# A hybrid decoder step on one Trainium2 core: first loads reordered, key copies moved, 512-column projections, 256 and 320 token columns

## Chip, cores and metric

The kernel runs as one program on one core of a Trainium2 chip. The metric is device time in microseconds of one execution. The profile is one execution, taken by the hardware profiler; its span runs from the first to the last instruction.

## The reference, cut to what matters

One layer of a decoder trunk is computed for 1024 prompt tokens and 64 sample tokens (8 sequences of 8), width 1024, FFN width 2816, all in float32.

```python
h = rmsnorm(x, norm_mix)
proj = h @ w_in                      # q/k/v for a gated DeltaNet, its gates, q/k/v for window attention
o_a = rmsnorm(gated_delta_rule(causal_conv(...)), norm_out_a) * silu(z)     # 4 heads of 128
o_b = rmsnorm(combine_by_denominator(dilated branches), norm_out_b)         # 8 heads of 64
x = x + concat([o_a, o_b]) @ w_out
hf = rmsnorm(x, norm_ffn)
x = x + (silu(hf @ w_gate) * (hf @ w_up)) @ w_down
y = rmsnorm(x, norm_final)
```

The sample tokens attend over a cache of 2048 keys and values per sequence. Among the outputs are the caches moved on by eight rows (`new_wk_sample`, `new_wv_sample`), 32 MB of copies each; part of them goes out from tiles that the attention has loaded, the rest as copies from DRAM to DRAM.

## The kernel before, in words

**Tokens and stages.** The prompt is cut into two groups G (or F in the second half of the kernel): group 0 has 512 prompt tokens, group 1 the other 512; the 64 sample tokens go with group 0 in the input projections and with group 1 in the output projection and the FFN. A tile of tokens is 128 rows; the sample tile has 64. The stages follow one another: norm and input projections (`norm_in`, `proj_a`, `proj_b`), the DeltaNet beside them, attention and the first half of the output projection (`outproj_a`, mixed heads 0 to 3), then `outproj_b(0)`, `ffn_norm(0)`, `ffn(0)` with attention of group 1 and the decode attention (`decode_k`, `decode_v`) beside it, and at the end `outproj_b(1)`, `ffn_norm(1)`, `ffn(1)`, alone but for copies.

**Matmuls.** Each float32 operand is split into a high and a low float32r part: `split` (lines 222 to 224) rounds on ScalarE and subtracts on VectorE. A product is then three matmuls: high by high, high by low, low by high, all issued on line 198. `dense_T` holds 128 weight columns still and streams n tokens, 24 matmuls of n columns for a depth of 1024. `nat_mm` holds 128 tokens still and streams weight columns, 12 matmuls for four blocks of depth (8 for the 64 sample tokens).

**Weights.** `wload` (line 226) loads 512 KB raw into one of two buffers (`WB`), `wsplit` (line 231) splits it into one of three high and three low buffers (`WH`, `WL`), or into four buffers of another pool when `own` is given.

**The FFN** (`ffn`, line 1261) goes over the 22 blocks of 128 FFN columns in groups of four (one group of two). Per block it loads gate and up weights and calls `dense_T` twice for each entry of `cols`: (0, 512) for F = 0, (0, 288) and (288, 288) for F = 1. From the two banks ScalarE and VectorE make the SwiGLU product (lines 1293 to 1298). After a group, `down` (line 1313) adds the group's product with `w_down` to the residual `x2` in SBUF: for each column part c and each token tile 12 matmuls into one PSUM bank, then one VectorE eviction on line 1320. For F = 0 and a group of four the column part is 256 wide (`ncol`), four parts; otherwise 512, two parts. `outproj_b` (line 1218) is built the same way, four parts of 256, its eviction on line 1238. In the stages up to the first FFN two banks (`m=2`) serve all these products; `ffn(1)` has six.

**The norm before the FFN** (`ffn_norm`, line 1250) goes by token tile through `norm_T` (line 284): a sum of squares on ScalarE (288), eight small VectorE steps (214 to 219), a scaled multiply (289), eight transposes on TensorE against the identity (294), two splits. The first norm of the kernel (`norm_in`) is the same with `wmix`.

**The order of work.** Generators yield estimated costs; `beside` takes turns between a main stream and side streams by a pace, so that matmuls of attention stand between those of the FFN. The framework then orders each engine's queue by priority and data, so that an instruction without predecessors may come far ahead of its place in the text: the eight copies of the last 512 key rows per sequence (line 1026, 1 MB each, issued by GpSimd, written inside `decode_k`) leave in the first 150 us.

**The first loads** (lines 1412 to 1418) go out on SP's queue in this order: two x tiles, the table of constants `tab` (520 KB, with the identity for transposes as its first 128 columns), `wmix` (one row broadcast to 128 partitions, 512 KB), the first weight, three more x tiles.

**The last copies.** `far_rows` (line 1338) copies the far part of a cache, 1.5 MB per sequence, from SP's queue in program order, beside `outproj_b(1)` and `ffn(1)` for the values, at a pace of 4.5 per copy and 0.3.

```python
            last, wide = f + nb == nf, F or nb == 2
            ncol = 512 if wide else 256
            parts = nb * ncol // 1024
            ...
    x0 = list(load_in(0, npl, range(2)))
    sp.dma_start(tab, C["table"])
    wbc = bcast_row(npl, I["norm_mix"], "wmix")
    raws = [(i, wload(in_cols(i), 8, 128)) for i in IN_ORDER[:E1]]
```

Of the kernel before, what the change touches and what calls it, by code (L numbers as in the profile page):

```python
# [86 lines left out]
def consts():  # L87
# [6 lines left out]
    t["ident"] = p == c  # L94
# [43 lines left out]
    return off, {"table": table, "wb": wb, "dbias": np.ascontiguousarray(db_all), "xin": xin}  # L138
# [8 lines left out]
def body(tc, I, O, C, off):  # L147
# [21 lines left out]
    def K(name):  # L169
        o, n = off[name]  # L170
        return tab[:, o:o + n]

    ident, ii, utri, ones = K("ident"), K("ii"), K("utri"), K("ones")
# [20 lines left out]
    def mbank():  # L194
        return bank("m", "pm")
# [795 lines left out]
    def decode_k(tp, pairs, kb=2, kt_=3, qb=2, pb=1):  # L991
# [23 lines left out]
        for pi in pairs:  # L1015
            S = tp.tile([96, 2, 64], F32, name="S", tag="S", bufs=1)
            pa = obank()
            for s in range(2):
                b = 2 * pi + s
                c16, o16, c4, o4, src = cache_rows(I["cache_win_k"], O["new_wk_sample"], b)  # L1020
                for j in range(4):
                    for i in range(2):
                        hs = slice(i * 64, i * 64 + 64)
                        nc.gpsimd.tensor_copy(qbd[hs, s, j, 2 * j + i::8], qf[hs, j, b * 8:(b + 1) * 8])
                n = PAST - 512
                pool_q.dma_start(O["new_wk_sample"][0, b, n - DS:PAST - DS].rearrange("(a e) h d -> a (e h d)", a=64),
                                 I["cache_win_k"][0, b, n:PAST].rearrange("(a e) h d -> a (e h d)", a=64))
# [192 lines left out]
    def outproj_b(F, tp, x2):  # L1220
# [11 lines left out]
        for c in range(4):  # L1232
            w = wsplit(w_out[:, 4:8, c * 256:(c + 1) * 256], 4, 256)
            for i, rows, col in toks(F):
                ps = mbank()[:, :256]
                nat_mm(his(hi), his(lo), w, 4, rows, col, ps, True, True)
                xv = x2[:, col // 128, c * 256:(c + 1) * 256]
                dve.tensor_tensor(xv, ps, xv, op=OP.add)  # L1238
                yield 1.3
# [21 lines left out]
    def ffn(F, tp, x2, hp):  # L1261
        cols = [(0, 288), (288, 288)] if F else [(0, 512)]
# [19 lines left out]
        while f < nf:  # L1282
# [3 lines left out]
            for j in range(nb):  # L1286
                wg = wsplit(w_g[:, :, (f + j) * 128:(f + j + 1) * 128], 8, 128)
                wu = wsplit(w_u[:, :, (f + j) * 128:(f + j + 1) * 128], 8, 128)
                for c0, n in cols:
                    pg = yield from dense_T(*wg, hi, lo, c0, n)  # L1290
                    pu = yield from dense_T(*wu, hi, lo, c0, n)
                    th = hp.tile([128, 512], F32, name="hth", bufs=2)[:, :n]
                    act.activation(th, pg[:, :n], AF.Tanh, scale=0.5)  # L1293
                    dve.scalar_tensor_tensor(th, th, 1.0, pg[:, :n], op0=OP.add, op1=OP.mult)
                    dve.tensor_tensor(th, th, pu[:, :n], op=OP.mult)
                    act.activation(hh[j][:, c0:c0 + n], th, AF.Copy, scale=0.5)
                    m = min(n, 512 - c0)
                    dve.scalar_tensor_tensor(hl[j][:, c0:c0 + m], th[:, :m], 0.5, hh[j][:, c0:c0 + m].bitcast(F32),
                                             op0=OP.mult, op1=OP.subtract)
                    if m < n:  # L1300
                        dve.scalar_tensor_tensor(hh[j][:, 576:640], th[:, m:n], 0.5, hh[j][:, 512:576].bitcast(F32),
                                                 op0=OP.mult, op1=OP.subtract)
                yield 0.1
            last, wide = f + nb == nf, F or nb == 2
            ncol = 512 if wide else 256
# [33 lines left out]
    def far_rows(c, o, new):  # L1339
# [5 lines left out]
        sp.dma_start(o[0, :, PAST - DS:PAST].rearrange("b t h d -> b t (h d)"), new.rearrange("(b t) f -> b t f", t=DS))  # L1345

# [66 lines left out]
    sp.dma_start(tab, C["table"])  # L1413
    wbc = bcast_row(npl, I["norm_mix"], "wmix")
    raws = [(i, wload(in_cols(i), 8, 128)) for i in IN_ORDER[:E1]]
    x0 += load_in(0, npl, range(2, 5))
    raws += [(i, wload(in_cols(i), 8, 128)) for i in IN_ORDER[E1:E2]]
# [74 lines left out]
    far = Side(far_rows(I["cache_win_v"], O["new_wv_sample"], smp[2]))  # L1492
# [31 lines left out]
```

## Time and profile before

| | us |
|---|---|
| median of 3 runs | 1782.13 (1782.08 to 1786.56) |
| the profiled execution, device time | 1786.49 |
| its span | 1784.7 |
| TensorE busy | 1697.0 (95%) |
| VectorE busy | 1150.2 (64%) |
| ScalarE busy | 679.4 (38%) |

All times below are microseconds from the start of the span unless another unit stands there. PE is TensorE's matmuls, PEld its weight loads, DVE is VectorE, ACT ScalarE, POOL GpSimd, SP the engine that only issues transfers; a q behind the name means the engine's queue of issues. A name such as x<-pm,x reads: tile x written from pm and x. In brackets stands how long the engine was idle before, and what ended the wait. The ends of matmuls are modelled, so that the distance between starts is the better measure of their cost.

### The profile page before, as it was taken

The page shows a single profiled execution, that of the slowest core. Times are in us where ns is not written, and L with a number is a line of the kernel's source. Part 1 is how long each engine was busy: PE and PEld are TensorE (multiplying, and loading weights), DVE is VectorE, ACT ScalarE, POOL GpSimd, SP SyncE. Part 2 cuts the span into 40 slices and gives each one's busy share as a digit, 9 for nine tenths or more (in the row PEclk, how much of TensorE's full clock was granted, in tenths as well). Part 3 has the DMA queues.
Part 4 walks back from the last instruction along what each step waited for, and adds up shares of the span by engine and source line. Part 5 has one row for each costly group of instructions (what it writes and reads, how often), then busy time and mean ns, then how long its engine had stood idle before and what let it go on. Part 6 is the DMA issues. An engine that isn't in the chain of part 4 may idle for free. (4 is left out here: it accounts for less than half of the span.)

```text
span 1784.7 us, 27958 instructions
## 1 busy us (share of the span) xinstructions
PE 1697.0 (95%) x10462; PEld 1464.7 (82%) x10462; DVE 1150.2 (64%) x2829; ACT 679.4 (38%) x1379; POOL 78.2 (4%) x200
## 2 busy tenths in 40 slices
PE   4999999997999999999999989999998999999997
PEld 4988789996766668878887778888887999999996
DVE  6978966866776757797666546676576444343435
ACT  4545434441423353676421134454234223131222
POOL 1000000001001000000011001111100000000000
PEclk9999999998999999999998999999998999999999
DMA  8645556468898867534299678798494333241321
GB/s 272 182 145 159 162 179 171 116 200 271 266 282 256 256 208 225 188 104 118 66 284 287 180 224 256 248 304 274 133 325 154 128 95 95 59 130 36 107 72 65
DMA packets 309569, 324.96 MB, mean 182 GB/s; under 512 B 28221, under 2 KB 260669, under 8 KB 307754
## 3 DMA queue, kind: packets, MB, share of 16 engines
q1 hardware_dynamic: 297754, 275.64, 51.6%
q0 software_dynamic: 10304, 43.08, 6.8%
q10 hardware_dynamic: 1376, 4.46, 0.7%
q8 instruction: 82, 1.34, 0.3%
q14 instruction: 53, 0.43, 0.1%
HBM read 251.31 MB, written 105.63 MB: 200 GB/s over the span
## 5 line engine op out<-in xcount | busy, mean ns | idle before, releaser
L198 PE MATMUL pm<-act_hi,whi 128*128 128x288 f32 (+1 forms) x1056 | 349.4, 331 | 0.2 <-ACT act_hi L223 0.2
L198 PE MATMUL pm<-act_lo,whi 128*128 128x288 f32 (+1 forms) x1056 | 348.1, 330 | 0.0
L198 PE MATMUL pm<-act_hi,wlo 128*128 128x288 f32 (+1 forms) x1056 | 347.4, 329 | 0.0
L223 ACT ACTIVATE whi<-wraw 128x1024 fp32r<-128x1024 f32 x182 | 192.8, 1059 | 381.8 <-PE pm L198 275.8
L224 DVE TENSOR_TENSOR wlo<-wraw,whi 128x1024 fp32r<-128x1024 f32 x182 | 222.3, 1222 | 123.8 <-ACT whi L223 123.3
L198 PE MATMUL pm<-xh,whi 128*128 128x320 f32 (+2 forms) x672 | 230.6, 343 | 11.5 <-ACT whi L223 8.6
L198 PE MATMUL pm<-xl,whi 128*128 128x320 f32 (+2 forms) x672 | 228.4, 340 | 0.1
L198 PE MATMUL pm<-xh,wlo 128*128 128x320 f32 (+2 forms) x672 | 226.7, 338 | 0.2
L198 PEld LDWEIGHTS pm<-act_hi,whi 128*128 128x128 f32 x1056 | 199.2, 189 | 18.4 <-issue 2.1
L198 PEld LDWEIGHTS pm<-act_hi,wlo 128*128 128x128 f32 x1056 | 199.3, 189 | 14.5 <-issue 0.5
L198 PEld LDWEIGHTS pm<-act_lo,whi 128*128 128x128 f32 x1056 | 199.3, 189 | 14.2 <-issue 0.2
L198 PEld LDWEIGHTS pm<-xh,whi 128*128 128x128 f32 x672 | 129.1, 192 | 25.9 <-ACT whi L223 9.1
L1320 DVE TENSOR_TENSOR x<-pm,x 128x256 f32<-128x256 f32 (+1 forms) x148 | 79.9, 543 | 98.2 <-PE pm L198 97.8
L198 PEld LDWEIGHTS pm<-xl,whi 128*128 128x128 f32 x672 | 129.0, 192 | 11.9 <-issue 3.2
L198 PEld LDWEIGHTS pm<-xh,wlo 128*128 128x128 f32 x672 | 128.7, 192 | 10.6 <-DVE wlo L224 1.5
L198 PE MATMUL pm<-own,hh 128*128 128x512 f32 x440 | 129.4, 390 | 0.0
L198 PE MATMUL pm<-whi,hh 128*128 128x256 f32 (+1 forms) x336 | 101.6, 303 | 12.9 <-DVE x L1320 7.6
L198 PE MATMUL pm<-whi,hl 128*128 128x256 f32 (+1 forms) x336 | 99.7, 299 | 0.0
L198 PE MATMUL pm<-wlo,hh 128*128 128x256 f32 (+1 forms) x336 | 99.4, 297 | 0.0
L198 PEld LDWEIGHTS pm<-own,hh 128*128 128x128 f32 x440 | 82.2, 188 | 16.9 <-issue 0.2
L198 PE MATMUL pm<-whi,nat_hi 128*128 128x256 f32 x288 | 83.4, 293 | 1.5 <-DVE n_ss L219 1.1
L1293 ACT ACTIVATE hth<-pm 128x288 f32<-128x288 f32 (+1 forms) x66 | 30.5, 462 | 139.4 <-PE pm L198 139.3
(362 smaller groups left out, 3180.9 us busy)
## 6 DMA issues: line engine op xcount, KB each, us to landing
wraw<-w_in SPq DMA_DIRECT2D x56, 512.0 KB, 4.6
wraw<-w_gate SPq DMA_DIRECT2D x44, 512.0 KB, 3.7
wraw<-w_up SPq DMA_DIRECT2D x44, 512.0 KB, 3.8
wraw<-w_down SPq DMA_DIRECT2D x44, 512.0 KB, 3.6
new_wk_sample<-cache_win_k SPq DMA_DIRECT2D x8, 1536.0 KB, 8.2
qbc<-smp SPq DMA_DIRECT2D x32, 384.0 KB, 7.2
kt<-cache_win_k SPq DMA_DIRECT2D x32, 384.0 KB, 7.0
vt<-cache_win_v SPq DMA_DIRECT2D x32, 384.0 KB, 4.2
```

What stands on the lines that cost most here:

```text
L198: pe.matmul(out, lhsT, rhs, start=start, stop=stop)
L223: act.activation(hi, src, AF.Copy)
L224: dve.tensor_sub(lo, src, hi.bitcast(F32))
L1293: act.activation(th, pg[:, :n], AF.Tanh, scale=0.5)
L1320: dve.tensor_tensor(xv, ps, xv, op=OP.add)
```

## The change

Four things are edited. The identity becomes a tensor and a load of its own, and the loads go out as x tiles, `wmix`, identity, first weight, x tiles, table. The eight key copies leave `decode_k` and GpSimd's queue and become a generator `near_keys` on SP's queue, in program order, behind the far values. The down projection always uses 512 columns, and `outproj_b` does too; a group of four blocks then takes its weights for one half in two pieces of two blocks. The second FFN cuts its tokens into 256 and 320, and its first group (two blocks) does both blocks for the first 256 tokens before the other 320, with the second block's weights in the pool's own buffers.

```diff
-    t["ident"] = p == c
...
-    ident, ii, utri, ones = K("ident"), K("ii"), K("utri"), K("ones")
+    ident = cp.tile([128, 128], F32, name="ident")
+    ii, utri, ones = K("ii"), K("utri"), K("ones")
...
-                n = PAST - 512
-                pool_q.dma_start(O["new_wk_sample"][0, b, n - DS:PAST - DS].rearrange("(a e) h d -> a (e h d)", a=64),
-                                 I["cache_win_k"][0, b, n:PAST].rearrange("(a e) h d -> a (e h d)", a=64))
...
-        for c in range(4):
-            w = wsplit(w_out[:, 4:8, c * 256:(c + 1) * 256], 4, 256)
+        for c in range(2):
+            cs = slice(c * 512, (c + 1) * 512)
+            w = [wsplit(w_out[:, k:k + 2, cs], 2, 512) for k in (4, 6)]
             for i, rows, col in toks(F):
-                ps = mbank()[:, :256]
-                nat_mm(his(hi), his(lo), w, 4, rows, col, ps, True, True)
-                xv = x2[:, col // 128, c * 256:(c + 1) * 256]
+                ps = mbank()
+                for q in range(2):
+                    nat_mm(his(hi), his(lo), w[q], 2, rows, col, ps, q == 0, q == 1, 2 * q)
+                xv = x2[:, col // 128, cs]
                 dve.tensor_tensor(xv, ps, xv, op=OP.add)
-                yield 1.3
+                yield 2.6
...
-        cols = [(0, 288), (288, 288)] if F else [(0, 512)]
+        cols = [(0, 256), (256, 320)] if F else [(0, 512)]
...
-            for j in range(nb):
-                wg = wsplit(w_g[:, :, (f + j) * 128:(f + j + 1) * 128], 8, 128)
-                wu = wsplit(w_u[:, :, (f + j) * 128:(f + j + 1) * 128], 8, 128)
-                for c0, n in cols:
...
+            early = F and f == 0
+            ws = {}
+            for j, (c0, n) in ([(j, c) for c in cols for j in range(nb)] if early else [(j, c) for j in range(nb) for c in cols]):
+                if j not in ws:
+                    ws = ws if early else {}
+                    ws[j] = [wsplit(x[:, :, (f + j) * 128:(f + j + 1) * 128], 8, 128, own=hp if early and j else None)
+                             for x in (w_g, w_u)]
+                wg, wu = ws[j]
+                pg = yield from dense_T(*wg, hi, lo, c0, n)
+                pu = yield from dense_T(*wu, hi, lo, c0, n)
...
-            last, wide = f + nb == nf, F or nb == 2
-            ncol = 512 if wide else 256
+            last, ncol = f + nb == nf, 512
...
+    def near_keys():
+
+        n = PAST - 512
+        for b in range(DB):
+            d_, s_ = (x[0, b, r:r + 512].rearrange("(a e) h d -> a (e h d)", a=64) for x, r in
+                      ((O["new_wk_sample"], n - DS), (I["cache_win_k"], n)))
+            tc.keep_in_program_order(sp.dma_start(d_, s_))
+            yield 4.5
...
     x0 = list(load_in(0, npl, range(2)))
-    sp.dma_start(tab, C["table"])
     wbc = bcast_row(npl, I["norm_mix"], "wmix")
+    sp.dma_start(ident, C["ident"])
     raws = [(i, wload(in_cols(i), 8, 128)) for i in IN_ORDER[:E1]]
     x0 += load_in(0, npl, range(2, 5))
+    sp.dma_start(tab, C["table"])
...
-    far = Side(far_rows(I["cache_win_v"], O["new_wv_sample"], smp[2]))
+    far = Side(far_rows(I["cache_win_v"], O["new_wv_sample"], smp[2]), near_keys())
```

## Rows read from the trace of the kernel before

**Rows 1.** The page: busy time of each engine, share of the span, instructions.
```profile
PE 1697.0 (95%) x10462; PEld 1464.7 (82%) x10462; DVE 1150.2 (64%) x2829; ACT 679.4 (38%) x1379; POOL 78.2 (4%) x200
```

**Rows 2.** Busy time by stage; columns: stretch, length, engines, clock, DMA share, GB/s.
```profile
0.00:18.50 18.50, 0.00 (x0) 0.00 (x0) 3.88 (x24) 3.58 (x5) 2.41 (x8) 1.00 0.89 319
...
760.00:820.00 60.00, 55.91 (x342) 45.55 (x342) 58.55 (x189) 42.88 (x88) 0.00 (x0) 1.00 0.41 119
880.00:1310.00 430.00, 414.82 (x2225) 345.12 (x2224) 266.94 (x399) 148.65 (x198) 47.07 (x110) 0.98 0.78 239
...
1336.50:1361.50 25.00, 15.43 (x91) 13.70 (x89) 22.32 (x59) 12.58 (x21) 0.95 (x1) 0.73 0.54 189
1361.50:1772.60 411.10, 411.05 (x2669) 387.15 (x2670) 179.95 (x306) 103.36 (x159) 0.00 (x0) 1.00 0.30 90
```

**Rows 3.** Timeline, 0 to 20; columns: start, time, engine, line, operation, tiles.
```profile
1.30 1.68 POOL L1026 DMA_DIRECT2D new_wk_sample<-cache_win_k  x3
...
2.13 0.43 SPq L300 DMA_DIRECT2D wmix<-norm_mix  x1
...
4.26 1.06 ACT L288 ACTIVATE xn<-xt 128x1024 f32<-128x1024 f32 x1 [2.25 <-DMA xt<-x_prompt]
...
8.10 0.16 DVE L219 SCALAR_TENSOR_TENSOR n_ss<-n_ss 128x1 f32<-128x1 f32 x1
...
17.23 1.28 DVE L289 SCALAR_TENSOR_TENSOR xn<-xt,n_ss,wmix 128x1024 f32<-128x1024 f32 x1 [8.97 <-DMA wmix<-norm_mix]
...
18.57 2.82 PE L294 MATMUL pn<-tab,xn 128*128 128x128 f32 x12 [18.57 <-DVE xn L289]
```

**Rows 4.** DMA queues, 4 to 13 (first two rows) and 15 to 21 (last).
```profile
q0 software_dynamic: 80, 3.15, 89.2%
q1 hardware_dynamic: 171, 0.64, 18.2%
...
q1 hardware_dynamic: 1453, 2.04, 99.8%
```

**Rows 5.** Timeline of TensorE in the first FFN, 1271 to 1276.
```profile
1271.75 0.28 PE L198 MATMUL pm<-whi,hh 128*128 128x256 f32 x1
...
1272.47 0.40 PE L198 MATMUL pm<-act_hi,whi 128*128 128x512 f32 x1
...
1275.90 0.39 PE L198 MATMUL pm<-act_hi,whi 128*128 128x512 f32 x1
```

**Rows 6.** Lines 1320 and 1295, 880 to 1310; waiters: us in all, times.
```profile
L1320 DVE TENSOR_TENSOR x<-pm,x x86: 406/424/692, 882.3 to 1309.0; 128x256 f32<-128x256 f32 x78, 128x512 f32<-128x512 f32 x8
...
  PE pm L198: 7.6, 3
...
  PE pm L198: 5.2, 2
```

**Rows 7.** Weight splits by form, 880 to 1310: count, busy, mean ns, idle before.
```profile
L224 DVE TENSOR_TENSOR wlo<-wraw,whi 128x1024 fp32r<-128x1024 f32 x57 | 69.6, 1220 | 25.4 <-ACT whi L223 25.3
...
L223 ACT ACTIVATE whi<-wraw 128x1024 fp32r<-128x1024 f32 x58 | 61.3, 1058 | 168.5 <-PE pm L198 126.1 <-issue 24.8 <-DMA wraw<-w_down 9.3
```

**Rows 8.** Timeline of VectorE and TensorE, a stall at 988 and the join.
```profile
988.81 1.22 DVE L1000 TENSOR_TENSOR pr<-kt,qbc 96x1024 f32<-96x1024 f32 x1 [3.68 <-DMA kt<-cache_win_k]
...
1335.05 0.15 DVE L214 TENSOR_SCALAR n_ss<-n_ss 128x1 f32<-128x1 f32 x1 [0.88 <-ACT xn L288]
...
1336.47 0.28 PE L198 MATMUL pm<-wlo,nat_hi 128*128 128x256 f32 x1
1338.54 1.09 PE L294 MATMUL pn<-tab,xn 128*128 128x128 f32 x8 [1.79 <-DVE xn L289]
...
1359.23 1.28 DVE L289 SCALAR_TENSOR_TENSOR xn<-x,n_ss,wffn 64x1024 f32<-64x1024 f32 x1
```

**Rows 9.** SP's issues in the second FFN; issues of the run with KB and us.
```profile
1380.67 1.12 SPq L1343 DMA_DIRECT2D new_wv_sample<-cache_win_v  x1
...
new_wv_sample<-cache_win_v SPq DMA_DIRECT2D x8, 1536.0 KB, 8.7
```

More of the change, by code (lines that the diff above doesn't have):

```diff
@@ L137, in consts @@
     xin = (rr == cc + 8 * (np.arange(128)[:, None, None] % 4)).astype(np.float32).reshape(128, 256)
-    return off, {"table": table, "wb": wb, "dbias": np.ascontiguousarray(db_all), "xin": xin}
+    return off, {"table": table, "ident": (p == c).astype(np.float32), "wb": wb, "dbias": np.ascontiguousarray(db_all), "xin": xin}
 def laid_out(cache_k):
@@ L1285, in ffn @@
             hl = [hp.tile([128, 512], F32R, name="hl", tag="hl", bufs=6) for _ in range(nb)]
-            for j in range(nb):
-                wg = wsplit(w_g[:, :, (f + j) * 128:(f + j + 1) * 128], 8, 128)
-                wu = wsplit(w_u[:, :, (f + j) * 128:(f + j + 1) * 128], 8, 128)
-                for c0, n in cols:
[L1290 to L1298, printed above, removed]
+            early = F and f == 0
@@ new lines, in ffn @@
+            ws = {}
[7 more added lines that the diff above has]
+                pu = yield from dense_T(*wu, hi, lo, c0, n)
+                th = hp.tile([128, 512], F32, name="hth", bufs=2)[:, :n]
+                act.activation(th, pg[:, :n], AF.Tanh, scale=0.5)
+                dve.scalar_tensor_tensor(th, th, 1.0, pg[:, :n], op0=OP.add, op1=OP.mult)
+                dve.tensor_tensor(th, th, pu[:, :n], op=OP.mult)
+                act.activation(hh[j][:, c0:c0 + n], th, AF.Copy, scale=0.5)
+                m = min(n, 512 - c0)
+                dve.scalar_tensor_tensor(hl[j][:, c0:c0 + m], th[:, :m], 0.5, hh[j][:, c0:c0 + m].bitcast(F32),
+                                         op0=OP.mult, op1=OP.subtract)
+                if m < n:
+                    dve.scalar_tensor_tensor(hh[j][:, 576:640], th[:, m:n], 0.5, hh[j][:, 512:576].bitcast(F32),
@@ L1299, in ffn @@
                                              op0=OP.mult, op1=OP.subtract)
-                    if m < n:
-                        dve.scalar_tensor_tensor(hh[j][:, 576:640], th[:, m:n], 0.5, hh[j][:, 512:576].bitcast(F32),
-                                                 op0=OP.mult, op1=OP.subtract)
                 yield 0.1
-            last, wide = f + nb == nf, F or nb == 2
-            ncol = 512 if wide else 256
+            last, ncol = f + nb == nf, 512
             parts = nb * ncol // 1024
```

## The prediction

> **What bounds the kernel now.** I read the page first: TensorE is busy 95% of the span, VectorE 64% [rows 1]. A busy TensorE is no proof that it is the bound everywhere, so I then cut the span into stages [rows 2]. In the second FFN (1361.5 to 1772.6) TensorE is busy 411.05 of 411.10 us at the full clock: only fewer or cheaper matmuls could shorten it. In the first FFN (880 to 1310) it is busy 414.8 of 430 us at a granted clock of 0.98. From 760 to 820 VectorE is the fuller one, 58.55 of 60 us. Two places are plainly empty: the first 18.5 us hold no matmul at all, and the 25 us between the last output-projection matmul and the steady second FFN have TensorE busy 15.4 us at a clock of 0.73, with VectorE busy 22.3 of 25. The change touches both empty places and the first FFN. So I read the start instruction by instruction [rows 3], the two DMA queues there [rows 4], the spacing of matmul starts at 256 and 512 columns [rows 5], who waits in the first FFN [rows 6], what a weight split takes [rows 7], and VectorE and TensorE at a stall and at the join into the second FFN [rows 8].
>
> **The start: -9.2 us.** VectorE has the first tile's scale ready at about 8.2 us (the Newton step at 8.10), then stands still until 17.23, where the wait ends on the landing of wmix; the first transpose is at 18.57 [rows 3]. wmix was issued at 2.13. What held it: between 4 and 13 us the software queue, on which GpSimd had issued three 1 MB key copies at 1.30, took 89.2% of the DMA engines and moved 3.15 MB, the hardware queue 0.64 MB in the same time [rows 4]. The change takes these copies out of the start, and lets two x tiles, wmix and the identity (512 + 512 + 512 + 64 KB, 1.64 MB) go ahead of everything; the 520 KB table follows five loads later. Alone the hardware queue moved 2.04 MB in the 6 us from 15 to 21, 339 GB/s [rows 4], so 1.64 MB takes 4.8 us. The first x tile was issued at 0.74 and used at 4.26 [rows 3]; its own 0.52 MB takes 1.5 us at that rate, which leaves 2.0 us before bytes flow. So wmix and identity stand at 0.74 + 2.0 + 4.8 = 7.5 us, before the scale at 8.2: the multiply starts near 8.0 to 8.3 in place of 17.23. I take 9.2 us. Above that nothing is to be had, for the x tiles themselves bound it (9.7); below, if later x tiles or the first weight become the wait, I keep 6. The identity adds one DMA issue on SP, 0.43 us like that of wmix; the rest of the table is first read for the gate columns after the first projection, so its later load is hidden by that projection's matmuls, and would cost its own 1.5 us if they were not there. The shift is carried through, since what follows is busy TensorE or VectorE work that waits on its predecessor and not on a date.
>
> **The copies at the end: 0.** Eight 1 MB issues leave GpSimd's queue (busy 4%) and go onto SP's queue behind the far value copies. Behind each stands the next weight load. The far copies are the nearest rows: 1.5 MB each, landing in 8.7 us, one of them issued at 1380.67 in the second FFN [rows 9], where TensorE lost 0.05 us in all [rows 2]. The stage uses 0.30 of the DMA engines. 8 MB more is hidden by those matmuls; bounds 0 (a stage with TensorE full has nothing to gain from a copy, and the five copies that leave the first projections are left at nothing too) and +8 (1 us per copy, if each should fall on loads of the down weights).
>
> The Trainium skill (DMA: Bandwidth & Descriptors, "Issuing engines are not separate DMA queues") says that DMAs of all engines run on the same 16 engines and interleave, so that issuing from another engine saves only issue time. By that, moving the copies to SP would gain nothing in itself, and the gain stands only in the place in time; rows 4 agree, with 89.2% going to the other queue.
>
> **512 columns in the first FFN's down projection and in the second half of the output projection: -8.2 us.** Five groups of four blocks each run 4 column quarters x 4 token tiles x 12 matmuls of 256 columns, 960 in all; after, 480 of 512. The output projection's half has 416 (192 + 224); after, 208.
> - Stream: 256 columns start every 0.120 us (six from 1271.75 to 1272.47), 512 every 0.2287 (fifteen from 1272.47 to 1275.90) [rows 5]. 480 x (0.240 - 0.2287) is 5.4 us; of the projection, which has less side work between its matmuls, I take half the difference, 208 x 0.0057 = 1.2. Together -6.6, bounds 2 and 8.
> - Waits for evictions: in the first FFN matmuls waited three times, 7.6 us in all, for an eviction, and twice, 5.2 us, for the SwiGLU product [rows 6]. They come when VectorE stands in a multiply that waits for a DMA, as for 3.68 us before 988.81 [rows 8]. There are two banks. One filled bank of cover is 12 x 0.12 = 1.4 us now, 2.75 after; each of three eviction waits shrinks by 1.1 us (the eviction grows from 0.42 to 0.69), and the last block's product, nine matmuls into the group, is wanted 1 us later in the two others. -5.3, bounds 0 and -9, the latter with the half-clock time that follows such waits (0.98 over 430 us is 17 us at the lower level).
> - VectorE between 760 and 820: 16 evictions of 0.42 become 8 of 0.69, -1.2 us on its path.
> - New: the weights come in two pieces per half, out of the same three buffers. The fourth piece of a group needs the buffer of the first, free only when the last token tile of the first half has passed its second block, 1.4 us before that half ends; it is wanted 1.4 us after. Its split is 1.06 us on ScalarE and then 1.22 on VectorE [rows 7], 2.3 against 2.8: just enough with an idle VectorE, 0.7 late behind one other operation. Seven such places (five groups, two projections): +4.9, bounds 0 and +14. While ScalarE's head waits for that buffer, side work of attention and decode queues behind it; I count that in the bound.
>
> The Trainium skill (TensorE: Matmul & The Clock Gate, "Back-to-back issue gap") gives N/2.4 ns plus 2.5 for a warm gap, 109 and 216 ns. By that a pair saves 2.5 ns and the stream term would be an estimated 1.7 us in place of 6.6. The rows show 120 and 229, so the fixed part is larger here, and the measurement decides.
>
> **256 and 320 columns, and the join: -6 us.** In steady flow nothing: 288 + 288 and 256 + 320 are the same columns in as many matmuls. What counts is the start. Of 25 us TensorE is idle 9.6, and a clock of 0.73 means 13.5 us at the lower level, 1.2 GHz, in which what work there was took twice its time; I put the loss at 9.6 + 3 = 12.6. VectorE began the first tile's norm at 1335.05, 1.4 us before the last projection matmul at 1336.47, and the last tile's multiply came at 1359.23 [rows 8]. Two edits help. With 512 columns the last pass over five token tiles is twice as long, so the first tile's x is ready 10.1 us before the projection's end and not 5.2: norms start 4.9 us earlier against it. And the first blocks ask for two token tiles, not three; four dense products of 24 x 0.12 = 11.5 us then cover the norms of the last three tiles. Against it stand two more weight splits (2 x 1.22) in the same VectorE stretch, which is the limit there: the last tile is ready some 19 to 21 us after the projection ends, with 14.8 us of TensorE work (11.5, and 24 transposes at eight in 1.09) to fill them. Lost after: 5 to 8; I take -6, bounds +3 (VectorE takes the added splits ahead of the norms, and TensorE stands again after the first 256 columns) and -11.
>
> **Sum.** -9.2 + 0 - 8.2 - 6 = -23.4 us. Against the profiled execution (span 1784.70, device time 1786.49) that is 1763.1. That execution is 4.4 us above the median of the runs; from the median, 1782.13, it is **1759 us**.
>
> **Rivals.**
> - Only the start is gained: the tight weight pieces give back the stream, and VectorE keeps the join as it is. 1782.1 - 9.2 = 1773. For it: VectorE's 22.3 of 25 us at the join; against: 40 fewer evictions. Chance 0.20.
> - More: TensorE no longer falls to the lower clock at the join and between down groups, -9.2 - 10 - 12 = 1751. Chance 0.16.
> - The copies meet the weights: while the copies ran at the start, the loads on SP's queue hardly moved [rows 4]. If each of the eight delays a down weight by 1 to 2 us of TensorE time, +8 to +16: 1768 to 1776, about 1774 with half the join lost. Chance 0.07.
> - Slower: the third weight buffer. Each of the seven places waits for the whole split behind a VectorE that itself stands 3.7 us on a DMA: 2.3 + 3.7 = 6, and the clock falls behind it, 3 more: 63 us, less 23.4 + 4.9 of the rest, is +35, 1817. It decides against the kernel from (28.3 + 5.3) / 7 = 4.8 us per place on. The longest VectorE stall I cite is 3.68 us, and seven such meetings are much. Chance 0.04.
> - The change does not do what it says at the start: the order of the loads is by need, yet the second x tiles or the first weight bind at once, half of that gain: 1764. Chance 0.05, within the range.
>
> **Numbers.** The forecast has 0.48. Range 1749 to 1774: it takes in the forecast, the start alone, the last case and the nearer half of the case of more. A measurement here tells about 0.3%, 5.3 us. Faster by more than that: all cases but the copies' and the slower one, 0.89; within it: most of the copies' case, if join and projections then give nothing beside it, 0.06; slower: the weight buffer and the rest of the copies' case, 0.05.
>
> **What would show it.** Right: first transpose near 9 us; no copy of keys before the second FFN; 512-column matmuls alone in the first FFN's down, its eviction wait under 5 us; no gap over 2 us in the middle of a down group with VectorE's wlo as releaser; lost time at the join under 9 us. Wrong: a first transpose after 12 us, a fall of the clock within the down groups, or waits of ScalarE for w_down in the second FFN that reach TensorE.

## The result: slower by 0.6%, and where the time went

The changed kernel takes 1797.02 us (median of 7 runs), the kernel before 1786.56 us in the same comparison: a ratio of 1.0061, 95% interval 1.0040 to 1.0081. The forecast was 1759 us and faster. The profiled execution of the changed kernel is its longest run (1804.33 us, span 1802.3), so stages are compared below and small differences are left alone. Medians are of the fast executions; one of run 2 (8928.11 us) and one of run 7 (2829.8 us) were slow and are left out.

Busy time by stage after the change (columns as in [rows 2]: stretch, length, PE, PEld, DVE, ACT, POOL, clock, DMA share, GB/s), then the same view of the kernel before for the two stages that [rows 2] does not cut:

```profile
0.00:18.50 18.50, 6.96 (x29) 6.03 (x30) 11.70 (x51) 9.91 (x16) 0.72 (x5) 1.00 0.84 264
380.00:490.00 110.00, 84.73 (x502) 70.80 (x503) 68.75 (x201) 31.95 (x91) 6.65 (x23) 0.89 0.71 219
760.00:820.00 60.00, 55.45 (x325) 45.01 (x324) 54.93 (x163) 42.91 (x88) 0.00 (x0) 0.97 0.34 102
880.00:1310.00 430.00, 422.03 (x1870) 329.16 (x1868) 276.86 (x385) 157.94 (x217) 47.66 (x110) 1.00 0.79 244
1338.80:1363.80 25.00, 22.20 (x163) 20.67 (x162) 22.40 (x54) 14.89 (x26) 0.95 (x1) 0.93 0.67 232
...
1440.00:1600.00 160.00, 145.72 (x876) 134.92 (x875) 55.55 (x86) 30.70 (x47) 0.00 (x0) 0.95 0.30 98
```

```profile
380.00:490.00 110.00, 97.88 (x607) 80.79 (x605) 77.12 (x253) 38.10 (x118) 7.75 (x26) 0.94 0.77 234
1440.00:1600.00 160.00, 160.00 (x1041) 150.69 (x1040) 67.51 (x107) 41.05 (x62) 0.00 (x0) 1.00 0.29 86
```

What the prediction aimed at was gained: TensorE works in the first 18.5 us, the first FFN is at 422 us of 430 and the full clock, the join at 22.2 of 25. Two stages that it did not touch lost: TensorE falls from 97.88 to 84.73 us busy in 380 to 490, and in the second FFN from 160.00 to 145.72 between 1440 and 1600. In lengths between the first matmuls of the stages, read off the timelines (us; the first column is the first transpose, the last one runs from the last down matmul of the first FFN to the last matmul of all):

| kernel | start | to first FFN | first FFN | to the end |
|---|---|---|---|---|
| before | 18.6 | 774.6 | 515.3 | 466.3 |
| after | 9.0 | 801.5 | 494.7 | 487.3 |

The stage table of the experiments goes on with these columns.

**The second FFN.** TensorE's timeline, then ScalarE's and SP's (SPq is its queue) over the same block; columns: start, time, engine, line, operation, idle time before it and what ended it:

```profile
1475.65 0.30 PE L198 MATMUL pm<-act_hi,wlo 128*128 128x320 f32 x1
1477.98 0.39 PE L198 MATMUL pm<-act_hi,whi 128*128 128x256 f32 x1 [2.03 <-ACT whi L223]
1478.20 0.28 PE L198 MATMUL pm<-act_lo,whi 128*128 128x256 f32 x1
1479.24 0.39 PE L198 MATMUL pm<-act_hi,wlo 128*128 128x256 f32 x1 [0.76 <-DVE wlo L224]
1479.46 0.37 PE L198 MATMUL pm<-act_hi,whi 128*128 128x256 f32 x1
```

```profile
1466.17 0.38 ACT L1297 ACTIVATE hth<-pm 128x256 f32<-128x256 f32 x1 [25.42 <-PE pm L198]
...
1472.54 0.44 ACT L1297 ACTIVATE hth<-pm 128x320 f32<-128x320 f32 x1 [2.71 <-PE pm L198]
1476.51 0.47 ACT L1300 ACTIVATE hh<-hth 128x320 fp32r<-128x320 f32 x1 [3.54 <-DVE hth L1299]
1476.89 1.99 ACT L223 ACTIVATE whi<-wraw 128x1024 fp32r<-128x1024 f32 x2
```

```profile
1457.87 0.38 SPq L228 DMA_DIRECT2D wraw<-w_gate  x1
1459.00 0.37 SPq L228 DMA_DIRECT2D wraw<-w_up  x1
1459.42 0.73 SPq L1356 DMA_DIRECT2D new_wk_sample<-cache_win_k  x1
```

At each of four blocks TensorE waits 2.03 us for the high split of the gate weight and 0.76 for its low one, and the matmuls after it start 0.21 apart instead of 0.120: the granted clock is then at its lower level, 1.2 GHz, for 3.4 us (6.8 behind one of the four). That is some 4.5 us a block (2.8 idle and half of 3.4), an estimated 20 us in all. Two more waits, 1.5 us for a split of `w_down` and 1.7 for a low split, bring TensorE's idle time from 1440 to 1600 to 14.3 us. The weights are not late. They were issued at 1457.87 and 1459.00. The view of the transfers from 1456 to 1470 gives the gate weight 3.7 us from issue to landing, which is 1461.6; between 1470 and 1480 nothing moves at all:

```profile
wraw<-w_gate SPq DMA_DIRECT2D x1, 512.0 KB, 3.7
```

```profile
DMA packets 0, 0.00 MB, mean 0 GB/s; under 512 B 0, under 2 KB 0, under 8 KB 0
```

So the gate weight lies ready for 15 us, in which ScalarE runs four instructions of 0.4 us and waits for matmuls and products, for in its queue the two splits come behind `hh` of the block before. There the order that the build fixed is: tanh, product, tanh, product, split, split (`hth<-pm` is the tanh, `hh<-hth` the product's copy). Before the change it was split, tanh, split, product, with a block's splits done while the block before still ran:

```profile
1415.80 1.06 ACT L223 ACTIVATE whi<-wraw 128x1024 fp32r<-128x1024 f32 x1 [2.10 <-PE pm L198]
1416.76 0.40 ACT L1293 ACTIVATE hth<-pm 128x288 f32<-128x288 f32 x1
1418.96 1.06 ACT L223 ACTIVATE whi<-wraw 128x1024 fp32r<-128x1024 f32 x1 [1.80 <-PE pm L198]
1419.92 0.43 ACT L1296 ACTIVATE hh<-hth 128x288 fp32r<-128x288 f32 x1
```

The pairs stand where key copies stand between the weight loads on SP's queue; the later blocks have the other order. The Trainium skill (TensorE: Matmul & The Clock Gate, in the paragraph on engine queue depths) calls the queues of ScalarE and VectorE strict FIFO, and the trace agrees: the splits start 0.38 us after `hh`, not when their data came.

**380 to 490.** One of the eight copies is not in the second FFN at all: it left at 388.26. SP's queue, then TensorE:

```profile
387.45 0.43 SPq L228 DMA_DIRECT2D wraw<-w_in  x1
388.26 0.56 SPq L1356 DMA_DIRECT2D new_wk_sample<-cache_win_k  x1
...
398.78 0.60 SPq L1346 DMA_DIRECT2D new_wk_sample<-cache_win_k  x1
422.01 0.35 SPq L597 DMA_DIRECT2D mix<-o  x1
...
432.35 0.43 SPq L228 DMA_DIRECT2D wraw<-w_in  x1
```

```profile
440.06 0.80 PE L198 MATMUL pm<-xh,whi 128*128 128x512 f32 x1 [16.66 <-ACT whi L223]
440.65 0.63 PE L198 MATMUL pm<-xl,whi 128*128 128x512 f32 x1
446.66 0.79 PE L198 MATMUL pm<-xh,wlo 128*128 128x512 f32 x1 [5.38 <-DVE wlo L224]
```

`keep_in_program_order` ties an instruction to the one written before it on its engine. For the first key copy that is the last transfer of `far_rows`, which stores the samples' new rows, is tied to nothing and may go early; it went at 371.8. So the copy went early behind it, and with it the order of this stage changed: SP stands 22.8 us at the `mix` store of a DeltaNet chunk, twelve issues stand between it and the next input weight, and that one goes at 432.35, as late as before (432.23), although TensorE was there 7 us sooner. From 400 to 424 the DMA engines are busy 0.35 of the time (0.75 in run 12), so the transfers are not full there. That the order and not the copy's bytes made this loss is read from the traces; no run parted the two here.

### The profile page after: what moved, and what is told of

Read it like the earlier page. It is cut to its first block, busy times and chain, and to the rows that moved or that the text cites. A ratio compares the mean times of both kernels' runs of the same rounds, so it can differ in the third digit from the quotient of the medians.

```text
span 1802.3 us, 26485 instructions
## 1 busy us (share of the span) xinstructions
PE 1701.2 (94%) x9774; PEld 1432.2 (79%) x9774; DVE 1149.2 (64%) x2771; ACT 676.3 (38%) x1379; POOL 76.1 (4%) x192
## 5 line engine op out<-in xcount | busy, mean ns | idle before, releaser
L198 PE MATMUL pm<-act_hi,whi 128*128 128x512 f32 (+2 forms) x1024 | 344.6, 337 | 11.4 <-ACT whi L223 8.1
L198 PE MATMUL pm<-act_hi,wlo 128*128 128x512 f32 (+2 forms) x1024 | 342.5, 335 | 4.7 <-DVE wlo L224 4.7
L198 PE MATMUL pm<-act_lo,whi 128*128 128x512 f32 (+2 forms) x1024 | 342.7, 335 | 0.1
L198 PE MATMUL pm<-xh,whi 128*128 128x320 f32 (+2 forms) x672 | 229.5, 342 | 19.5 <-ACT whi L223 16.7
L1323 DVE TENSOR_TENSOR x<-pm,x 128x512 f32<-128x512 f32 x108 | 74.2, 689 | 94.4 <-PE pm L198 94.1
L198 PEld LDWEIGHTS pm<-own,hh 128*128 128x128 f32 x440 | 82.3, 188 | 18.8 <-DVE own L224 1.9
L1297 ACT ACTIVATE hth<-pm 128x256 f32<-128x256 f32 (+2 forms) x66 | 30.5, 462 | 139.7 <-PE pm L198 139.7
L1299 DVE TENSOR_TENSOR hth<-hth,pm 128x256 f32<-128x256 f32 (+2 forms) x66 | 34.9, 529 | 69.9 <-PE pm L198 69.8
L198 PE MATMUL pm<-whi,nat_hi 128*128 128x256 f32 (+1 forms) x216 | 72.6, 339 | 5.6 <-ACT whi L223 3.2
L224 DVE TENSOR_TENSOR vl<-vt,vh 96x1024 fp32r<-96x1024 f32 (+1 forms) x48 | 58.3, 1218 | 24.9 <-ACT vh L223 24.8
L223 ACT ACTIVATE vh<-vt 96x1024 fp32r<-96x1024 f32 (+1 forms) x48 | 50.6, 1057 | 60.7 <-PE po L198 50.8
```

The costliest lines, as they stand in the source:

```text
L198: pe.matmul(out, lhsT, rhs, start=start, stop=stop)
L223: act.activation(hi, src, AF.Copy)
L224: dve.tensor_sub(lo, src, hi.bitcast(F32))
```

## The experiments

Ratios are to the kernel before in the same comparison, with 95% intervals. First the stages of every profile:

| kernel | start | to first FFN | first FFN | to the end |
|---|---|---|---|---|
| without copies | 9.2 | 780.5 | 497.6 | 464.9 |
| copies put back | 18.1 | 776.5 | 495.9 | 463.7 |
| transfer in front pinned | 9.1 | 784.8 | 493.8 | 495.4 |
| ScalarE's queue | 9.0 | 781.4 | 490.7 | 469.8 |
| other shape | 9.2 | 787.7 | 490.3 | 465.2 |
| pinned in the key pass | 9.0 | 794.6 | 519.8 | 463.8 |
| order alone | 9.1 | 779.1 | 493.3 | 476.2 |
| columns alone | 19.1 | 774.1 | 495.3 | 468.6 |
| cut alone | 18.9 | 772.7 | 514.9 | 462.1 |
| copies alone | 10.4 | 774.2 | 516.3 | 467.5 |
| GpSimd late | 9.0 | 776.4 | 491.5 | 484.3 |
| behind a weight | 9.2 | 781.9 | 496.5 | 462.3 |

**1. Without the copies.** Is it the copies, or one of the other parts?

```diff
-    far = Side(far_rows(I["cache_win_v"], O["new_wv_sample"], smp[2]), near_keys())
+    far = Side(far_rows(I["cache_win_v"], O["new_wv_sample"], smp[2]))
```

> The changed kernel without the eight copies of the near keys, which leaves out 512 rows of each sequence's new_wk_sample; all else of the change stays. Theory A (the eight copies stand between the weight loads on SP's in-order queue, so the weights' splits fall in pairs behind the SwiGLU work on ScalarE, and TensorE waits some 3.4 us at each block of the second FFN from 1440 to 1580; the first copy, which slipped out to 388 us, is the cause of the late weight at 423 to 440 too): both losses go, 1797 - 24 - 12 to 18 = 1755 to 1761 us. Theory B (the copies cost the second FFN only; the late weight at 423 to 440 is the order of the DeltaNet's transfers on SP's queue, which the earlier start meets, with or without the slipped copy): 1797 - 24 = 1773 us, with a gap of over 15 us near 423 still there. Rival C (the cut into 256 and 320 columns makes the gaps of the second FFN): 1795 to 1797 us, the gaps near 1475, 1493 and 1510 stay.

1759.09 us, ratio 0.9816 (0.9773 to 0.9859). Both losses are gone: "to the first FFN" falls by 21 us, the end by 22, TensorE is busy 160.00 of 160 us from 1440 on, and near 423 a gap of 8.2 us is left, where the kernel before has one of 8.6 near 431. Theory A holds, B and C fall.

**2. The copies put back** into the key pass on GpSimd's queue, the other three parts kept.

```diff
+                n = PAST - 512
+                pool_q.dma_start(O["new_wk_sample"][0, b, n - DS:PAST - DS].rearrange("(a e) h d -> a (e h d)", a=64),
+                                 I["cache_win_k"][0, b, n:PAST].rearrange("(a e) h d -> a (e h d)", a=64))
                 for r in range(0, 512, 256):
```

> The changed kernel with the eight copies put back where the kernel before has them, in the samples' key pass on GpSimd's queue; the other three parts stay. Theory A: the second FFN as without copies, the late weight at 423 to 440 gone, what the copies cost in the key pass within 3 us: 1756 to 1764 us. Theory B: the second FFN without gaps of over 2 us, the late weight still there: 1773 to 1776 us. Rival C: 1795 to 1797 us.

1760.52 us, ratio 0.9850 (0.9812 to 0.9887): theory A again. Its start is that of the kernel before, with the new order of the first loads in it:

```profile
16.80 1.28 DVE L289 SCALAR_TENSOR_TENSOR xn<-xt,n_ss,wmix 128x1024 f32<-128x1024 f32 x1 [8.76 <-DMA wmix<-norm_mix]
18.14 1.97 PE L294 MATMUL pn<-ident,xn 128*128 128x128 f32 x8 [18.14 <-DVE xn L289]
```

With the copies in place the order of the loads is worth 0.4 us; the rest of the start belongs to the copies.

**3. The transfer in front pinned**, so that no copy slips out.

```diff
-        sp.dma_start(o[0, :, PAST - DS:PAST].rearrange("b t h d -> b t (h d)"), new.rearrange("(b t) f -> b t f", t=DS))
+        tc.keep_in_program_order(
+            sp.dma_start(o[0, :, PAST - DS:PAST].rearrange("b t h d -> b t (h d)"), new.rearrange("(b t) f -> b t f", t=DS)))
```

> The changed kernel with the one unpinned transfer in front of the copies (the samples' new rows, the last of far_rows) kept in program order as well, so that all eight key copies go in the second FFN and none at 388 us. Theory A: the stage of 380 to 480 us gets 12 to 18 us back, the second FFN keeps its gaps and gets one copy more: 1779 to 1787 us. Theory B: the gap near 423 stays, and one copy more stands in the second FFN: 1797 to 1801 us.

1793.79 us, ratio 1.0036 (1.0014 to 1.0058). The stages say what theory A says: 16.7 us come back ahead of the first FFN, and with eight copies instead of seven in the second FFN 8 more are lost there. The time itself fell by less than expected and its interval overlaps that of the changed kernel, so this rests on two profiles and on run 12.

**4. ScalarE's queue** for the same copies.

```diff
-            tc.keep_in_program_order(sp.dma_start(d_, s_))
+            tc.keep_in_program_order(act.dma_start(d_, s_))
```

> The changed kernel with the eight copies issued in program order from ScalarE in place of SP: the same bytes at about the same time, but none of them ahead of a weight load on SP's queue. If the loss of the second FFN is one of order on SP's queue (theories A and B): at most two gaps of over 2 us between 1400 and 1600 and 18 to 24 us less there, so within 6 us of the run without copies. Rival D (the copies take the transfers' bandwidth from the weights, whatever queue they are on): the gaps of 1440 to 1580 stay to over half, 1785 us or more where the run without copies has 1773.

1761.69 us, ratio 0.9842 (0.9810 to 0.9875). Four waits of TensorE, 4.1 us together, are left between 1400 and 1600, at a higher DMA share (0.37 against 0.30). Rival D falls: the same bytes in the same stage cost 3 us more than no copies by the medians, 5 by the last stage.

**5. Another shape**, on SP's queue, at the same places of the program; the transfer in front is pinned as in run 3.

```diff
-            d_, s_ = (x[0, b, r:r + 512].rearrange("(a e) h d -> a (e h d)", a=64) for x, r in
+            d_, s_ = (x[0, b, r:r + 512].rearrange("(a e) h d -> a e (h d)", a=128) for x, r in
                       ((O["new_wk_sample"], n - DS), (I["cache_win_k"], n)))
-            tc.keep_in_program_order(sp.dma_start(d_, s_))
+            for e in (0, 2):
+                tc.keep_in_program_order(sp.dma_start(d_[:, e:e + 2], s_[:, e:e + 2]))
```

> The changed kernel, complete, with the eight key copies at the same places of SP's queue in the second FFN (and the one in front pinned, so that none slips out), but each issued as two transfers of 128 rows of 4 KB in place of one of 16 rows of 64 KB. Bytes, queue and place stay; what differs is the order that the build fixes on ScalarE, where the splits of the second FFN's weights now stand between tanh and the product's copy in nearly every block, not in pairs behind it. Theory E (the loss is that fixed order on ScalarE, not a late weight: at 1476.89 us the split of weights issued at 1457.87 and 1459.00 only begins, with the transfers idle from 1470 on): at most three gaps of over 1 us between 1400 and 1600, second FFN within 5 us of the run without copies, 1759 to 1765 us. Theory F (a copy of 1 MB ahead of a weight load on SP's queue holds the load up on the chip): the gaps of 1440 to 1580 stay, 1780 us or more.

1764.44 us, ratio 0.9886 (0.9841 to 0.9931); against run 3, from which only the shape differs, 1.5% less. TensorE is busy 160.00 us of 1440 to 1600. ScalarE in one block:

```profile
1469.14 1.06 ACT L223 ACTIVATE whi<-wraw 128x1024 fp32r<-128x1024 f32 x1 [2.51 <-PE pm L198]
1470.10 0.42 ACT L1297 ACTIVATE hth<-pm 128x320 f32<-128x320 f32 x1
1472.66 1.06 ACT L223 ACTIVATE whi<-wraw 128x1024 fp32r<-128x1024 f32 x1 [2.13 <-PE pm L198]
1473.62 0.46 ACT L1300 ACTIVATE hh<-hth 128x320 fp32r<-128x320 f32 x1
```

With the same bytes between the weight loads of the same stage the splits stand between tanh and product, and the view of TensorE's waits is empty there. Theory F falls. Why the build orders differently for the other shape was not tried; that its estimate of the transfer's time differs is only the likely reading.

**6. Pinned in the key pass**: run 2 with each copy in program order on GpSimd.

```diff
-                pool_q.dma_start(O["new_wk_sample"][0, b, n - DS:PAST - DS].rearrange(...), I["cache_win_k"][0, b, n:PAST].rearrange(...))
+                tc.keep_in_program_order(
+                    pool_q.dma_start(O["new_wk_sample"][0, b, n - DS:PAST - DS].rearrange(...), I["cache_win_k"][0, b, n:PAST].rearrange(...)))
```

> The changed kernel with the copies back in the samples' key pass on GpSimd's queue, as in the run with the copies put back, but kept in program order there, so that none can leave at the start (where that run has its first transpose at 18.1 us, as the kernel before at 18.57, with the new order of the first loads). If the copies alone hold up the start: first transpose at 9 to 9.5 us. The time: 4 to 9 us less than with the copies put back, 1754 to 1759 us, if the 1 MB copies are hidden in the key pass; rival: they meet the key tiles' loads there (DMA share 0.70 to 0.82 in those stages) and give it back, 1762 to 1770 us.

1792.27 us, ratio 1.0038 (1.0007 to 1.0070). The start is 9.0 us, as expected; the time is far above even the rival's range. The first FFN is 24 us longer than with the copies at the start (run 2), and the way to it 18 us longer, twice what the start gained. VectorE's waits in it, columns: who for whom, us in all, times, longest:

```profile
DVE hth L1303 <- PE pm L198: 22.4, 11, 4.5
DVE pr L1000 <- DMA kt<-cache_win_k: 21.0, 5, 7.4
DVE pr L1000 <- DMA qbc<-smp: 7.9, 2, 6.5
```

VectorE stands up to 7.4 us in the key pass's multiply for a key tile (at most 3.8 in run 2), and TensorE waits 9.7 us in all for SwiGLU products. Order and transfers were not told apart here.

**7. The order alone**, on run 1.

```diff
-        split(hi, lo, raw)
+        x = act.activation(hi, raw, AF.Copy)
+        if late:
+            tc.keep_in_program_order(x)
+        dve.tensor_sub(lo, raw, hi.bitcast(F32))
...
+                                    late=F and f + j in (6, 7, 8, 9, 10))
```

> The run without copies (512 rows of each sequence's new_wk_sample left out), with one thing added: the splits of five blocks' weights in the second FFN (blocks 6 to 10) are kept in program order on ScalarE, behind the product's copy of the block before, which is the order that the changed kernel shows there. No copy, no byte more. Theory E (order on ScalarE): each of the five blocks loses 3.4 us in two gaps (2.33 and 1.04 us between starts, 2.8 of it idle) and 1.7 us by the half clock behind it, 15 to 22 us more than the run without copies, 1774 to 1781 us. Theory F (the copies hold up the loads on the chip): under 3 us more, 1757 to 1762 us.

1770.10 us, ratio 0.9915 (0.9874 to 0.9955): 11 us more than run 1 by the medians, 11.3 more by the last stage; its interval and that of run 1 do not overlap. TensorE's waits between 1400 and 1600, all of them (us in all, times, longest):

```profile
PE pm L198 <- ACT whi L238: 7.4, 6, 2.0
```

At three of the five blocks TensorE waits 2.03 us for the gate's high split, as it did in the changed kernel, and then 0.45 for the other weight's, each time with 3.4 us at the lower clock behind it, without a copy in the program; at the other two the trace shows no such wait. With three blocks for five that is under the expected 15 to 22 us, and far over theory F's 3.

**8. The columns alone**, on the kernel before: the diff's edits of `outproj_b` and of `ncol`.

```diff
-            last, wide = f + nb == nf, F or nb == 2
-            ncol = 512 if wide else 256
+            last, ncol = f + nb == nf, 512
```

> The kernel before with one part of the change alone: 512 columns in the first FFN's down projection and in the second half of the output projection. The prediction's term: 8.2 us less than the kernel before (stream 6.6, eviction waits 5.3, VectorE 1.2, third weight buffer +4.9). Rival, by the stages of the two profiles (first down group to last: 412 us with the copies put back, 436 before; the output projection's end 6 us of that back): 14 to 18 us less. If the third weight buffer decides: 0 to 4 us less.

1766.16 us, ratio 0.9881 (0.9840 to 0.9921), 21 us less (14 to 29). The eviction in the first FFN, where [rows 6] had TensorE waiting 7.6 us:

```profile
L1321 DVE TENSOR_TENSOR x<-pm,x x48: 676/691/692, 883.5 to 1289.3; 128x512 f32<-128x512 f32 x48
its engine sat idle before it (us, times) until:
  PE pm L198: 27.1, 20
who waited for it (us, times):
  POOL new_wv_sample L1110: 1.0, 1
```

No matmul waits for it any more.

**9. The cut alone**, on the kernel before.

```diff
-        cols = [(0, 288), (288, 288)] if F else [(0, 512)]
+        cols = [(0, 256), (256, 320)] if F else [(0, 512)]
...
+            early = F and f == 0
```

> The kernel before with one part of the change alone: the second FFN's tokens as 256 and 320, the first two blocks in the new order with their weights in buffers of their own. The prediction's term: 6 us less than the kernel before. By the profiles (last matmul 1757.1 with the 512 columns alone, 1754.2 with all but the copies' move, whose difference is this part and the order of the first loads): 3 us less. Rival (the 320-column work, or the added splits, costs as much as the join gains): within 2 us of before.

1781.97 us, ratio 0.9976 (0.9958 to 0.9993): 4.3 us less (1.2 to 7.5), and 4.2 by the last stage, between term and reading.

**10. The copies alone**, on the kernel before: out of `decode_k`, and `near_keys` in the form of run 12.

> The kernel before with the move of the copies alone, in the form that cost nothing in the second FFN (two transfers of 128 rows each on SP, the first one pinned behind a weight load so that none slips out); the first loads keep their old order, the table ahead. First transpose: the prediction's mechanism (the copies on GpSimd's queue starve the first loads) gives 9 to 11 us in place of 18.57, where the loads' new order gave 0.5 us with the copies left in place. The time: if the shift is carried through, as the prediction put it, 7.5 to 9 us less than before; if it is swallowed where the DeltaNet's chain and the weights meet near 423 us and by the reordering behind it (with the copies moved or put back, the last matmuls of the complete forms differ by 2 us), 2 to 4 us less.

1779.70 us, ratio 0.9971 (0.9949 to 0.9994): 5.2 us less (1.1 to 9.1). The first multiply and transpose, for [rows 3]:

```profile
9.05 1.29 DVE L289 SCALAR_TENSOR_TENSOR xn<-xt,n_ss,wmix 128x1024 f32<-128x1024 f32 x1 [0.44 <-DMA wmix<-norm_mix]
...
10.39 2.82 PE L294 MATMUL pn<-tab,xn 128*128 128x128 f32 x12 [10.39 <-DVE xn L289]
```

8.2 us earlier with the table still ahead of `wmix`. In its profile the stage to the first FFN keeps its length, so the shift is carried through to there; by the end 6.5 us of it are left. The interval holds both expectations.

**11. GpSimd late**: the changed kernel's copies on GpSimd's queue.

```diff
-            tc.keep_in_program_order(sp.dma_start(d_, s_))
+            tc.keep_in_program_order(pool_q.dma_start(d_, s_))
```

> The changed kernel, complete, with the eight copies in program order on GpSimd's queue at the point where the change has them: nothing that any engine waits for is queued behind them there, but nothing spaces them either, so all eight leave one behind the other once GpSimd has cleared the last tile's zeros, at about 1325 to 1345 us, into the loads of the join. The orders on SP and ScalarE are those of the run without copies. If only order counts: 1757 to 1762 us. Rival D (8 MB at once starve the weights, as three such copies did at the start, when the hardware queue moved 0.64 MB in 9 us): a wait of TensorE for a weight of 10 us or more between 1325 and 1380, 1768 to 1780 us.

1774.88 us, ratio 0.9930 (0.9901 to 0.9959): rival D, for a burst. GpSimd's queue, the two DMA queues between 1330 and 1360 (packets, MB, share), and the wait behind them:

```profile
1325.78 3.91 POOL L1356 DMA_DIRECT2D new_wk_sample<-cache_win_k  x8
```

```profile
q0 software_dynamic: 240, 7.34, 71.7%
q1 hardware_dynamic: 2285, 2.57, 28.3%
```

```profile
ACT whi L223 <- DMA wraw<-w_gate: 26.7, 2, 23.6
```

One split waits 23.6 us for its weight, `hh` of a block before stands behind it on ScalarE, and TensorE loses 16 us in two waits for `hh`:

```profile
PE pm L198 <- ACT hh L1300: 16.0, 2, 12.8
```

So transfers do cost when eight leave together, and little or nothing when they are spread: the last stage is 469.8, 465.2 and 462.3 us in runs 4, 5 and 12, and 464.9 without copies.

**12. Behind a weight**: run 5's transfers, with the pause ahead of each copy, so that the first is tied to a weight load of the second FFN; `far_rows` as it was.

```diff
         for b in range(DB):
+            yield 4.5
             d_, s_ = (x[0, b, r:r + 512].rearrange("(a e) h d -> a e (h d)", a=128) for x, r in
                       ((O["new_wk_sample"], n - DS), (I["cache_win_k"], n)))
             for e in (0, 2):
                 tc.keep_in_program_order(sp.dma_start(d_[:, e:e + 2], s_[:, e:e + 2]))
-            yield 4.5
```

> The changed kernel, complete, with the eight copies on SP's queue in the second FFN as two transfers of 128 rows each, the first pinned behind a weight load of the second FFN (the generator pauses before each copy and not after it), so that the stages ahead of it keep the order of the run without copies. Theory E: the stage of 380 to 490 as without copies (one gap of 8 to 9 us, 10 us at half clock, no 23.9 us at half clock as where the transfer in front was pinned), the second FFN without gaps of over 2 us: 1757 to 1763 us, about 25 us less than the kernel before.

1757.81 us (5 runs), ratio 0.9832 (0.9802 to 0.9861): complete, some 30 us less than the kernel before by the ratio, and 39 less than the median of the change as it was made.

```profile
380.00:490.00 110.00, 97.32 (x588) 78.58 (x587) 78.31 (x253) 37.46 (x117) 8.69 (x27) 0.94 0.83 251
...
1440.00:1600.00 160.00, 160.00 (x1037) 150.40 (x1037) 65.41 (x103) 37.48 (x56) 0.00 (x0) 1.00 0.36 112
```

Both stages stand as in the kernel before. Its profile is 42.7 us shorter than that of the changed kernel: 19.6 to the first FFN, 25.0 behind it, less 1.8 in it.

## Why the prediction was wrong, point by point

**The copies at the end: 0, bounds 0 and +8. This step failed.** They cost 38 us (1797.02 against 1759.09 without them, run 1), in two places. The prediction asked whether the bytes have room and whether a copy delays a weight on its way, and took the far value copies as the nearest rows [rows 9]. The bytes do have room. What it left out is that moving an instruction onto an in-order queue changes the order that the build fixes on the other engines: splits behind products, which make most of the 22 to 25 us lost in the second FFN (against runs 1 and 12; runs 5 and 7 are the proof from both sides), and one copy that was not tied where the text has it, worth 17 to 21 us by the first FFN (runs 3, 12 and 1). The nearest row was near in bytes and not in what it did to the order: the far copies, 96 rows of 16 KB each, left the splits alone. The rival "the copies meet the weights" looked at the right place, but with the wrong cause and price (1 to 2 us a copy, 0.07): in the block shown the gate weight lay ready for 15 us, and each of four blocks lost about 4.5 us.

**"No copy of keys before the second FFN"** was listed as what would show the step right; the copy at 388.26 showed it wrong. The other signs listed came as named: the first transpose at 8.97, no matmul waiting for the eviction in the first FFN, no gap with VectorE's `wlo` in a down group there, a join with under 9 us lost.

**The start: -9.2.** The mechanism held: first transpose at 8.97 us, 9.6 earlier, and runs 2 and 10 show that the copies made it. The load order gave 0.4 with the copies in place, and a little over 1 us without them (10.4 in run 10, 9.0 to 9.2 with both edits). "The shift is carried through" is not settled: run 10 alone, 8.2 us earlier at the start, ends 5.2 earlier (1.1 to 9.1), which allows it; in runs 1 and 12, with the other parts, the stage up to the first FFN is 6 to 7 us longer than in the kernel before and swallows most of it.

**512 columns: -8.2, measured -21 (run 8). Too small, and in its waits.** The first FFN's stage is 20.0 us shorter. TensorE's idle time in it falls from 16.1 to 6.9 us, chiefly since the eviction waits are gone (7.6 to 0), and its time at the lower clock by 17 us (20.5 to 3.4), which is worth half of that. Together that is 17.7 us, and what is left, 2 to 3 us, is the stream's, where the prediction had 5.4 for this part. The prediction had put the waits at 5.3 with an upper bound of 9 and the clock in the bound: that is the term that was too small. Of the seven places in the term of +4.9 for the third weight buffer at most one is seen: TensorE waits once, 3.7 us, for `whi` in the output projection of run 8 (3.1 in run 12).

**256 and 320: -6, measured -4.3 (run 9),** inside its bounds. With the 512 columns the join is fuller than either part makes it: over the 25 us behind the projection TensorE is busy 21.6 us at the full clock in run 12, 18.8 at a clock of 0.86 with the columns alone (run 8), 17.5 at 0.86 with the cut alone (run 9), 15.4 at 0.73 before [rows 2].

**The sum.** The three parts measured alone give 21.2 + 4.3 + 5.2 = 30.7 us by their ratios, and run 12, which has all of them, 30.0 (25 to 35); with intervals of 3 to 7 us to either side of each part the sum is no close test. That run 12 stands at the forecast 1759 us is partly chance: terms of 9.2, 8.2 and 6 came out as 5, 21 and 4.

**The rule of the Trainium skill** that was weighed there (DMA: Bandwidth & Descriptors, "Issuing engines are not separate DMA queues") says that the issuing engine saves only issue time. For the transfers run 4 agrees: from ScalarE's queue a copy lands 7.4 us after its issue at the median, and 7.2 in the one case known from SP's. For the kernel the issuing engine was worth 35 us between that run and the change as made, since it decides in whose order a copy stands.

## What to carry to other kernels

Before pricing a moved transfer at its bytes, compare the built order of every in-order engine with the one before, and look for consumers that moved behind other work: data that lie ready while the engine waits are the sign. Tie a copy to an instruction that is itself held in place, never to one that is free, and read in the trace where the first one really left. In these runs transfers without consumers cost nothing that can be seen when spread behind weight loads (runs 5 and 12), and 16 us when eight leave at once (run 11).

## What was not expected of the hardware

Two queues did not share the DMA engines evenly by bytes. In run 2, between 4 and 13 us:

```profile
q0 software_dynamic: 80, 3.15, 93.0%
q1 hardware_dynamic: 184, 0.68, 20.6%
```

The hardware queue gets 2.3 times the packets and a fifth of the bytes. In the trace 48 of the copies' 80 packets are of 64 KB and 166 of the loads' 184 of 4 KB; the others are of 4 bytes. The Trainium skill (DMA: Bandwidth & Descriptors, "Queues, rings and completion order") has each engine take turns between queues by packets; turns of such unequal packets would give unequal bytes, and so much agrees with the trace. The turns themselves it does not show: 166 data packets went beside 48, not as many, and whether the profile's packets are the skill's is open. Whether a copy of another shape takes less from the loads beside it was not tried at the start.
